# Expert products at one width: 64 slots as two times 32, and another order of the eight expert places

## The chip, the cores and the metric

The kernel runs on one core of a Trainium2 chip. The metric is device time in microseconds for one execution; the kernel before takes 1484.67 us as the median of three runs.

## The reference

A two-layer encoder trunk over 256 tokens of 1024 features, in f32, conditioned by one vector. Layer 0 has two kinds of attention side by side and a dense SwiGLU. Layer 1 has a dilated window attention and then eight routed experts, of which each token takes two. Only the experts matter here:

```python
logits = jnp.einsum('td,de->te', xt, router)
top_val, top_idx = lax.top_k(logits, 2)
gates = jax.nn.softmax(top_val, axis=-1)
...
xb = xt[tok]                                   # the tokens that chose expert e
yb = (jax.nn.silu(xb @ wg[e]) * (xb @ wu[e])) @ wd[e]     # 1024 -> 3584 -> 1024
...
y = jnp.zeros_like(xt).at[tok_pad].add(yb * g)
```

With 256 tokens and two choices each there are 512 token slots over eight experts, some 64 for each. The weights of one expert are 3 x 1024 x 3584 f32 values, 44 MB.

## The kernel before

The stages follow one another: modulation vectors, layer 0 attention, dense FFN, layer 1 projection (`project`, products 128 slots wide and 512 columns long that go to two PSUM banks in turn, three to each, through `mm3`, L331 to L333), dilated attention, routing, and from about 518 us the experts. The dense FFN of layer 0 uses `mm3` too, with 256 columns to a product.

The experts are worked off in eight **places**. Expert 7 (`FIRST`) is always in place 0. The other seven are ranked on the chip by how many tokens chose them, and `RANK` says which rank goes to which place. The three experts with the fewest tokens (ranks 0 to 2) have **small places**, with room for 64 slots (`TWO`); the other five have **large places**, with room for 96 (`ROOM`). Tokens beyond the room would go to `overflow`, behind a condition at the end (L1343 to L1356). The weights of a place are found with a register that holds the expert's number, so the program is the same for any routing.

Places are gathered in pairs (0,1), (2,3), (4,5), (6,7): `route` (L1234) builds one-hot matrices `oh`, multiplies the tokens `htok` by them (L1251) into `xg`, with the token slots of both places side by side, and makes the gates and row numbers for the way back (L1265 to L1268). The route of the next pair is written into the second place of a pair (`ahead`, in the code at the 18th of the down products).

Within a place the weights come as 42 slots of 1 MB, 28 for gate and up and 14 for down; each slot is two **granules** of 128 x 1024 values. SyncE issues the loads in the order of use. They go round a ring of 16 slots (`RING` 8, `RING2` 2, `RING4` 4, `RING3` 2); a load is issued when PE is done with the slot's granules before.

The token slots are PE's stationary operand and the weights the moving one. PE's array of 128 columns is split: a product of 64 token slots uses 64 of its columns, two such products (at `tile_position` 0 and 64) take two pieces of the granule; a product of 32 slots uses 32, and four of them (at 0, 32, 64, 96) take four pieces. `parts` (L1229) says that a small place is `(0, 64, 2)`, 64 slots in two pieces of 512 columns, and that a large place has `(64, 32, 4)` as well, the further 32 slots in four pieces of 256 columns. `products` (L1278) issues them granule by granule. The operands are f32; each product shows in the trace as two records, and each has its own weight load (PEld).

Gate and up have 7 groups of 8 granules (`for g`, `for k`). At the end of a group ScalarE (silu, L1310) and VectorE (product, L1311) make `hh`; `turn` (L1286) transposes it on PE (L1292, two transposes in a small place, three in a large one) and ScalarE and VectorE copy it to `ht` for the down products. In the code the turn of group g-1 stands after the fourth granule of group g. At the end of a place `scatter` (L1322) scales the result (L1327) and adds it to the output in DRAM by an indirect DMA from GpSimd (L1328): one for the first 64 slots, a second one for the further 32 of a large place. The two write the same output, so each waits for the one before.

The order on each engine isn't that of the code line by line: the framework that builds the program schedules ready instructions by priority, with its own assumptions on durations. The trace shows what came of it.

The modulation vectors come from `gemv_mm` (L311, products at L315): four products at a time, 32 columns of the array each, 512 columns of weights long.

Of the kernel before, what the change touches and what calls it, by code (L numbers as in the profile page):

```python
# [22 lines left out]
NE = 8  # L23
EPS = 1e-6
BIG = 4096.0
TWO = (1, 3, 5)
FIRST = NE - 1
RANK = (-1, 0, 3, 1, 4, 2, 5, 6)
ROOM = tuple(64 if j in TWO else 96 for j in range(NE))
RING = 8  # L30
NCONV = 3
# [148 lines left out]
def tile_trunk(ctx, tc, xT_d, fm_d, rw_d, ct_d, ada_et, ada_e, win_ab, win_c, uq_d, ukv_d, wout_e,  # L180
               ffn_gu, ffn_d, ada_ot, ada_o, qkv_d, wout_o, router_d, gu_d, wd_d, out, dbg=None):
    nc = tc.nc
    V, S, G, TE = nc.vector, nc.scalar, nc.gpsimd, nc.tensor
# [9 lines left out]
    def bank(tag):  # L193
        return psum.tile([P, 512], F32, tag=tag, name="ps" + tag, bufs={"A": 2, "D": 1, "B": 3, "C": 2}[tag])
# [40 lines left out]
    def F(n):  # L235
        return fm[:, FM[n][0]:FM[n][1]]
# [28 lines left out]
    for a in range(2):  # L265
        ps = bank("C")
        for b in range(4):
            k = 4 * a + b
# [490 lines left out]
    for a in range(3):  # L759
        g = F("qn")[:, a:a + 1] if a < 2 else F("kvn")  # L760
# [31 lines left out]
    for tt in range(2):  # L792
        for a in range(2):
            ps = bank("B")
# [6 lines left out]
    at = ExitStack()  # L801
# [88 lines left out]
    for f in range(22):  # L890
        ps = bank("A").rearrange("p (a b) -> p a b", a=2)
# [89 lines left out]
    at = ExitStack()  # L981
# [58 lines left out]
    def granules(j):  # L1040

        for make in [gu_load(j, g, kq) for g in range(7) for kq in range(4)] + [wd_load(j, pc) for pc in range(14)]:
            w = make()
            for lo in (0, 1024):
                yield w[:, lo:lo + 1024]
# [72 lines left out]
    rk8 = mb.tile([P, NE], F32, name="rk8")  # L1118
    for j, r in enumerate(RANK):
        G.memset(rt8[:, j:j + 1], float(r))  # L1120
# [3 lines left out]
    ps = bank("C")  # L1124
# [73 lines left out]
    def gates():  # L1198
# [14 lines left out]
        V.tensor_copy(eid, key)  # L1213
        V.tensor_scalar(cap, rk8, float(len(TWO)) - 0.5, -32.0, op0=ALU.is_lt, op1=ALU.mult)
        V.tensor_scalar(cap[:, :NR], cap[:, :NR], 96.0, None, op0=ALU.add)
# [13 lines left out]
    def parts(e):  # L1229


        return ((0, 64, 2),) if e in TWO else ((0, 64, 2), (64, 32, 4))

# [38 lines left out]
    def expert(e, xg, lo, mid, ahead):  # L1272


        wg = granules(e)
        hh, hts = {}, {}

        def products(outs, x, w, m, start, stop):  # L1278
            for ps, (at, n, q) in zip(outs, parts(e)):
                c = 1024 // m // q  # L1280
                wv = w.rearrange("p (m c) -> p m c", m=m)
                for j in range(q):
                    TE.matmul(ps[n * j:n * j + n, :m * c].rearrange("p (m c) -> p m c", m=m), x(at, n),  # L1283
                              wv[:, :, j * c:(j + 1) * c], start=start, stop=stop, tile_position=(0, n * j))

        def turn(g):  # L1286

            h = hh.pop(g)
            pt = bank("C")
            nb = 2 if e in TWO else 3  # L1290
            for b in range(nb):
                TE.transpose(pt[:, b * P:(b + 1) * P], h[:, b * P:(b + 1) * P], ident)  # L1292
            ht = mt.tile([P, 4, 96], F32, tag="ht%d" % g, name="ht")
            S.copy(ht[:, :, 0:64].rearrange("p (j b) t -> p b j t", b=2),  # L1294
                   pt[:, 0:256].rearrange("p (b j t) -> p b j t", b=2, j=2))
            if nb == 3:
                V.tensor_copy(ht[:, :, 64:96], pt[:, 256:384].rearrange("p (j t) -> p j t", j=4))  # L1297
            hts[g] = ht

        for g in range(7):  # L1300
            ps = [bank("A"), bank("B")][:len(parts(e))]
            for k in range(KD):
                products(ps, lambda at, n: xg[:, k, lo + at:lo + at + n], next(wg), 2, k == 0, k == KD - 1)
                if g and k == 3:
                    turn(g - 1)
                if g == 0 and k == 3 and mid:
                    mid()
            h = mt.tile([P, 384], F32, tag="hh", name="hh", bufs=2)
            for p, (at, w) in zip(ps, ((0, 256), (256, 128))):
                S.activation(h[:, at:at + w], p[:, 0:w], AF.Silu)  # L1310
                V.tensor_tensor(h[:, at:at + w], h[:, at:at + w], p[:, w:2 * w], op=ALU.mult)  # L1311
            hh[g] = h
        Y = [bank("D"), bank("B")][:len(parts(e))]
        for c in range(28):
            if c == 18 and ahead:
                ahead()
            products(Y, lambda at, n: hts[c // 4][:, c % 4, at:at + n], next(wg), 1, c == 0, c == 27)
            if c == 2:
                turn(6)
        return Y  # L1320
# [13 lines left out]
    for e in range(NE):  # L1334
        if e % 2 == 0:
            xg, at, back = nxt.pop()
        ahead = (lambda: nxt.append(route(e + 1))) if e % 2 and e + 1 < NE else None
        scatter(e, expert(e, xg, at[e % 2], None if e else g5_sum, ahead), back[e % 2])
# [104 lines left out]
```

## Time and profile before

| | |
|---|---|
| three runs | 1484.15, 1484.67, 1487.27 us; median 1484.67 |
| profiled execution | 1487.64 us; its span in the trace 1485.8 us |
| mean granted TensorE clock | 0.984 |
| PE products | 1418.4 us busy, 95% of the span, 9779 records |
| PE weight loads (PEld) | 647.5 us, 44%, 9779 records |
| VectorE, ScalarE, GpSimd | 433.6, 354.2, 51.1 us |
| read from HBM | 467.34 MB, mean 317 GB/s |

The profile shows one execution. Times of rows are microseconds from the start of the span; durations of single groups are in ns. PE is TensorE's products, PEld its weight loads, DVE VectorE, ACT ScalarE, POOL GpSimd, SP SyncE; a q behind it is the engine's sequencer. Products are pipelined, so a record is longer than the distance to the next one's start: the starts are what tells the pace. An x with a number is a count of records that a row merges.

### The profile page before, as it was taken

The page shows a single profiled execution, that of the slowest core. Times are in us where ns is not written, and L with a number is a line of the kernel's source. Part 1 is how long each engine was busy: PE and PEld are TensorE (multiplying, and loading weights), DVE is VectorE, ACT ScalarE, POOL GpSimd, SP SyncE. Part 2 cuts the span into 40 slices and gives each one's busy share as a digit, 9 for nine tenths or more (in the row PEclk, how much of TensorE's full clock was granted, in tenths as well). Part 3 has the DMA queues.
Part 4 walks back from the last instruction along what each step waited for, and adds up shares of the span by engine and source line. Part 5 has one row for each costly group of instructions (what it writes and reads, how often), then busy time and mean ns, then how long its engine had stood idle before and what let it go on. Part 6 is the DMA issues. An engine that isn't in the chain of part 4 may idle for free.

```text
span 1485.8 us, 23384 instructions
## 1 busy us (share of the span) xinstructions
PE 1418.4 (95%) x9779; PEld 647.5 (44%) x9779; DVE 433.6 (29%) x964; ACT 354.2 (24%) x750; POOL 51.1 (3%) x51
## 2 busy tenths in 40 slices
PE   6889999999989899999999998999998999999996
PEld 4646999998766722223322222322222322222221
DVE  5866787786886410000000000000000000000000
ACT  4557644445568310000100001100000100000000
POOL 0320000000020000000000000000000000000000
PEclk9989999999999899999999999999999999999998
DMA  9846678788432788999999999999999999999830
GB/s 393 341 155 251 212 285 299 284 306 308 161 114 91 295 336 321 320 331 415 421 418 420 378 331 419 421 417 421 351 333 410 421 414 421 367 326 335 317 140 11
DMA packets 67363, 472.11 MB, mean 318 GB/s; under 512 B 8145, under 2 KB 8593, under 8 KB 11185
## 3 DMA queue, kind: packets, MB, share of 16 engines
q1 hardware_dynamic: 64944, 467.34, 81.5%
q0 software_dynamic: 1872, 2.10, 0.9%
q8 instruction: 79, 1.29, 0.3%
q10 hardware_dynamic: 432, 1.08, 0.2%
q14 instruction: 36, 0.29, 0.1%
HBM read 467.34 MB, written 3.80 MB: 317 GB/s over the span
## 4 chain that ended last, share of the span: by engine, by line
issue 51%; PE 34%; DMA 7%; DVE 5%; ACT 2%; POOL 0%; POOLq 0%; SPq 0%; ACTq 0%; DVEq 0%
DMA out_dram<-acc,row 7%; PE psA L331 6%; PE psA L332 6%; PE psA L333 6%; PE psA L1283 4%; PE psB L1283 3%; PE psD L1283 2%; DVE wlo L355 1%; PE psD L610 1%; PE psB L315 1%; PE psC L596 1%; PE psB L562 1%; PE psA L562 1%; DMA w<-in_ada_ot_dram 1%; PE psC L1251 0%
## 5 line engine op out<-in xcount | busy, mean ns | idle before, releaser
L1283 PE MATMUL psA<-w,xg 128*64 128x512 f32 x1792 | 453.3, 612 | 0.0
L1283 PE MATMUL psD<-w,ht 128*64 128x512 f32 x896 | 229.3, 611 | 0.0
L1283 PEld LDWEIGHTS psA<-w,xg 128*64 128x64 f32 x1792 | 102.3, 136 | 196.9 <-issue 180.1
L1283 PE MATMUL psB<-w,xg 128*32 128x256 f32 x2240 | 180.8, 393 | 0.0
L1310 ACT ACTIVATE hh<-psA 128x256 f32<-128x256 f32 x56 | 21.5, 384 | 603.3 <-PE psA L1283 603.3
L355 DVE TENSOR_TENSOR wlo<-w,whi 128x1024 fp32r<-128x1024 f32 (+2 forms) x119 | 143.8, 1214 | 44.1 <-ACT whi L353 44.1
L1311 DVE TENSOR_TENSOR hh<-hh,psA 128x256 f32<-128x256 f32 x56 | 23.6, 421 | 452.2 <-ACT hh L1310 452.2
L1283 PEld LDWEIGHTS psB<-w,xg 128*32 128x32 f32 x2240 | 44.4, 108 | 227.7 <-issue 227.7
L353 ACT CAST whi<-w 128x1024 fp32r<-128x1024 f32 (+2 forms) x119 | 122.2, 1038 | 74.1 <-issue 30.0
L331 PE MATMUL psA<-h,whi 128*128 128x256 f32 x352 | 97.1, 277 | 0.2 <-ACT h L455 0.2
L332 PE MATMUL psA<-h,whi 128*128 128x256 f32 x352 | 97.1, 277 | 0.0
L333 PE MATMUL psA<-h,wlo 128*128 128x256 f32 x352 | 96.8, 276 | 0.0
L1283 PE MATMUL psB<-w,ht 128*32 128x256 f32 x1120 | 89.5, 391 | 0.0
L1283 PEld LDWEIGHTS psD<-w,ht 128*64 128x64 f32 x896 | 49.6, 135 | 90.2 <-issue 86.9
L1283 PEld LDWEIGHTS psB<-w,ht 128*32 128x32 f32 x1120 | 22.0, 108 | 113.6 <-issue 109.5
L1327 DVE SCALAR_TENSOR_TENSOR acc<-psD,gsl,g5a 128x512 f32<-128x512 f32 x8 | 6.0, 751 | 224.3 <-PE psD L1283 224.3
L331 PEld LDWEIGHTS psA<-h,whi 128*128 128x128 f32 x352 | 66.0, 188 | 0.6 <-ACT h L455 0.4
L332 PEld LDWEIGHTS psA<-h,whi 128*128 128x128 f32 x352 | 65.9, 188 | 0.3 <-DVE h L456 0.2
L333 PEld LDWEIGHTS psA<-h,wlo 128*128 128x128 f32 x352 | 65.9, 188 | 0.0
L1294 ACT COPY ht<-psC 128x256 f32<-128x256 f32 x56 | 20.9, 372 | 169.7 <-PE psC L1292 169.7
L1328 POOL DMA_INDIRECT out_dram<-acc,row x13 | 20.2, 1557 | 959.0 <-DVE acc L1327 923.4
L1297 DVE COPY ht<-psC 128x128 f32<-128x128 f32 x35 | 10.2, 292 | 141.6 <-ACT ht L1294 141.6
(335 smaller groups left out, 1583.5 us busy)
## 6 DMA issues: line engine op xcount, KB each, us to landing
w<-in_gu_dram SPq DMA_DIRECT2D x224, 1024.0 KB, 10.8
w<-in_wd_dram SPq DMA_DIRECT2D x112, 1024.0 KB, 11.1
w<-in_ada_e_dram SPq DMA_DIRECT2D x22, 1024.0 KB, 8.9
w<-in_ffn_gu_dram SPq DMA_DIRECT2D x22, 1024.0 KB, 5.1
w<-in_ada_ot_dram SPq DMA_DIRECT2D x16, 1024.0 KB, 4.9
w<-in_qkv_dram SPq DMA_DIRECT2D x12, 1024.0 KB, 6.6
w<-in_ffn_d_dram SPq DMA_DIRECT2D x11, 1024.0 KB, 6.6
w<-in_ada_o_dram SPq DMA_DIRECT2D x8, 1024.0 KB, 6.3
```

The costliest lines, as they stand in the source:

```text
L315: behind(TE.matmul(ps[32 * j:32 * j + 32], sc[:, 4 * i + j], w[:, j], start=i == 0, stop=i == 1, tile_position=(0, 32 * j)), after)
L331: TE.matmul(out_, a[0], b[0], start=start, stop=False)
L332: TE.matmul(out_, a[0], b[1], start=False, stop=False)
L333: TE.matmul(out_, a[1], b[0], start=False, stop=stop)
L353: behind(S.copy(hi[:, :n], w), self.after[0])
L355: self.last = V.tensor_tensor(lw, w, hi[:, :n].bitcast(F32), op=ALU.subtract)
L562: TE.matmul(bk[i][:, tt], q[:, tt * P:(tt + 1) * P], k, start=True, stop=True)
L1283: TE.matmul(ps[n * j:n * j + n, :m * c].rearrange("p (m c) -> p m c", m=m), x(at, n), wv[:, :, j * c:(j + 1) * c], start=start, stop=stop, ...
L1294: S.copy(ht[:, :, 0:64].rearrange("p (j b) t -> p b j t", b=2), pt[:, 0:256].rearrange("p (b j t) -> p b j t", b=2, j=2))
L1310: S.activation(h[:, at:at + w], p[:, 0:w], AF.Silu)
L1311: V.tensor_tensor(h[:, at:at + w], h[:, at:at + w], p[:, w:2 * w], op=ALU.mult)
L1328: G.indirect_dma_start(out=out.rearrange("t (j c) -> (t j) c", j=q), out_offset=bass.IndirectOffsetOnAxis(ap=row[:, 0:1], axis=0), in_=ys, ...
```

## The change

The small places move from 1, 3 and 5 to 1, 4 and 7. The ranks move with them, so that the three experts with the fewest tokens are still the ones in small places. In large places the first 64 slots are no longer multiplied as one product of 64 per piece, but as two products of 32 on the same piece of the weights, at neighbouring positions: four products of 512 columns at 0, 32, 64, 96, and then, as before, four of 256 columns. Small places keep their two products of 64. The turn of the group before stands one granule later in the code.

```diff
-TWO = (1, 3, 5)
+TWO = (1, 4, 7)
 FIRST = NE - 1
-RANK = (-1, 0, 3, 1, 4, 2, 5, 6)
+RANK = (-1, 0, 3, 4, 1, 5, 6, 2)
 ...
             for ps, (at, n, q) in zip(outs, parts(e)):
                 c = 1024 // m // q
                 wv = w.rearrange("p (m c) -> p m c", m=m)
+                b = n if e in TWO else 32
                 for j in range(q):
-                    TE.matmul(ps[n * j:n * j + n, :m * c].rearrange("p (m c) -> p m c", m=m), x(at, n),
-                              wv[:, :, j * c:(j + 1) * c], start=start, stop=stop, tile_position=(0, n * j))
+                    for i in range(0, n, b):
+                        o = n * j + i
+                        TE.matmul(ps[o:o + b, :m * c].rearrange("p (m c) -> p m c", m=m), x(at + i, b),
+                                  wv[:, :, j * c:(j + 1) * c], start=start, stop=stop, tile_position=(0, o))
 ...
-                if g and k == 3:
+                if g and k == 4:
                     turn(g - 1)
```

## Rows read from the trace of the kernel before

**Rows 1.** The page's list of engines: busy us, share of the span, records.
```profile
PE 1418.4 (95%) x9779; PEld 647.5 (44%) x9779; DVE 433.6 (29%) x964; ACT 354.2 (24%) x750; POOL 51.1 (3%) x51
```

**Rows 2.** Windows of places 0, 1, 2, 3, 7: length, busy, clock, DMA share, GB/s.
```profile
518.40:661.30 142.90, 142.90 (x1063) 33.99 (x1061) 10.04 (x31) 12.07 (x33) 0.00 (x0) 0.97 0.91 329
661.30:749.00 87.70, 83.32 (x420) 29.50 (x418) 4.66 (x16) 9.11 (x25) 3.27 (x2) 1.00 1.01 409
749.00:884.90 135.90, 135.90 (x1033) 31.96 (x1029) 8.23 (x23) 7.24 (x21) 1.54 (x1) 1.00 0.99 389
884.90:975.30 90.40, 83.19 (x418) 29.49 (x416) 4.70 (x16) 9.10 (x25) 3.09 (x2) 1.00 1.01 413
...
1337.60:1473.50 135.90, 135.90 (x1033) 31.97 (x1029) 8.10 (x24) 7.24 (x21) 3.09 (x2) 1.00 0.61 215
```

**Rows 3.** Waits of PE and PEld, 661 to 1474 us: total us, times, longest.
```profile
PE psC L1292 <- DVE hh L1311: 15.1, 16, 0.9
...
PEld psA L1283 <- DMA w<-in_gu_dram: 3.8, 12, 0.4
```

**Rows 4.** Timeline of PE in place 2: start, length, instruction, records merged.
```profile
761.56 1.08 PE L1283 MATMUL psA<-w,xg 128*64 128x512 f32 x4
...
762.04 0.60 PE L1283 MATMUL psA<-w,xg 128*64 128x512 f32 x2
...
762.57 0.64 PE L1283 MATMUL psB<-w,xg 128*32 128x256 f32 x8
...
762.80 0.40 PE L1283 MATMUL psB<-w,xg 128*32 128x256 f32 x4
763.13 1.08 PE L1283 MATMUL psA<-w,xg 128*64 128x512 f32 x4
764.14 0.64 PE L1283 MATMUL psB<-w,xg 128*32 128x256 f32 x8
764.71 0.55 PE L1292 MATMUL psC<-fm,hh 128*128 128x128 f32 x3
765.19 1.08 PE L1283 MATMUL psA<-w,xg 128*64 128x512 f32 x4
```

**Rows 5.** Timeline of PE in place 3, the first group and its transposes.
```profile
884.87 7.09 PE L1283 MATMUL psA<-w,xg 128*64 128x512 f32 x32
892.90 0.44 PE L1292 MATMUL psC<-fm,hh 128*128 128x128 f32 x2 [0.94 <-DVE hh L1311]
```

**Rows 6.** Timeline of PE in the layer-1 projection, across a change of bank.
```profile
360.16 0.39 PE L333 MATMUL psA<-whi,h 128*128 128x512 f32 x1
360.38 0.39 PE L331 MATMUL psA<-whi,h 128*128 128x512 f32 x1
```

**Rows 7.** Timeline of PE in the modulation products ahead of the experts.
```profile
501.93 2.78 PE L315 MATMUL psA<-w,sc 128*32 128x512 f32 x24
```

**Rows 8.** Timeline of PE, the gathering among the down products of place 3.
```profile
948.17 0.79 PE L1251 MATMUL psC<-oh,htok 128*128 128x160 f32 x5
...
950.76 0.79 PE L1251 MATMUL psC<-oh,htok 128*128 128x160 f32 x5
```

**Rows 9.** Windows within place 1: with scatters under way, and after them.
```profile
661.30:673.00 11.70, 11.70 (x59) 3.87 (x57) 1.08 (x3) 0.76 (x2) 1.73 (x1) 1.00 0.96 333
...
700.00:749.00 49.00, 46.35 (x248) 17.70 (x250) 2.00 (x10) 5.69 (x16) 0.00 (x0) 1.00 1.01 421
```

**Rows 10.** The chain that ended last, and the timeline of POOL, at the end.
```profile
1474.09 5.85 DMA out_dram<-acc,row
...
1480.69 1.54 POOL L1328 DMA_INDIRECT out_dram<-acc,row  x1 [5.06 <-DMA out_dram<-acc,row]
```

**Rows 11.** Windows in the dense FFN and late in place 5: records of PE, PEld.
```profile
211.00:225.00 14.00, 14.00 (x126) 14.00 (x126) 11.06 (x18) 6.80 (x11) 0.00 (x0) 1.00 0.80 285
...
1188.90:1193.10 4.20, 4.03 (x64) 1.89 (x60) 0.47 (x3) 1.28 (x5) 0.00 (x0) 1.00 1.02 423
```

## The prediction

> **What bounds the kernel now.** I read the busy times first: PE works 95% of the span, no other engine a third of it [rows 1]. Then the expert stage by windows, one window for each of the eight places. The places follow one another without gaps from 518.4 to 1473.5 us, 955 of the 1485.8 us, and they come in two kinds. A large place (0, 2, 7, and 4 and 6 like them) takes 135.9 us, place 0 with its start 142.9; a small one (1, 3, and 5 like it) takes 87.7 or 90.4 [rows 2]. In large places PE is busy from end to end and the weights arrive at 389 GB/s or less, in place 7 at 215, because nothing is left to load; in small places they arrive at 409 to 413. So I looked at who waits: in the whole stage PE waits for weights a few times for 0.4 us, and in small places some 16 times 0.9 us for the activations in front of a transpose [rows 3]. The bound is PE, and in a large place it is PE's own stream.
>
> Next that stream. A granule is one half of a loaded slot (128 rows by 1024 columns, 0.524 MB). A large place passes it as two products 64 slots wide and 512 columns long, then four products 32 wide and 256 long; each product shows as two records. The first records start at 761.56, the second pair at 762.04, the 32-wide ones at 762.57, their second four at 762.80, the next granule at 763.13 [rows 4]. PE's granted clock is 1.00 in all places but the first (0.97) [rows 2]. So products at different column positions run together ("a round"), and the four rounds of a granule last 0.48, 0.53, 0.23 and 0.33 us: 1.57 us.
>
> Now the same 64-wide products in a small place, where nothing else is between them: 32 records, 16 rounds, take 7.09 us; less the 0.6 us of the last record that is 0.43 us for a round [rows 5]. So a round of 512 columns that costs 0.43 in an even stream costs 0.48 and 0.53 in a large place. The loss stands where the width changes. What else changes there is the PSUM bank. But in the layer-1 projection the bank changes after every third product, at equal width (128), and the next one starts the usual 0.22 us later, between a third product (L333) and the next first (L331) [rows 6]. Hence the width.
>
> **The change: the stream of the five large places.** After it, all products of a large place are 32 wide: per granule two rounds of four with 512 columns and two rounds of four with 256. Is a round of four as quick as a round of two? The modulation products (L315) are just that, 32 wide, 512 long, four positions: 24 records, six rounds, take 2.78 us [rows 7]; less 0.6 for the last record that is 0.43 a round. So 2 x 0.43. A 256-column round in an even stream isn't in the trace. Lower bound: half of 0.43, 0.215; upper bound: 0.24, rounded up from the 0.23 of the first round of a pair, which holds a restart [rows 4]. I take 0.215, because rounds scale with columns (512 columns cost 0.43 both at two and at four positions). Granule: 0.86 + 0.43 = 1.29 us, with the upper bound 1.34.
>
> The transposes (turn) still change the width, once into them and once out. In a large place they stand after the second granule of the next group, not after the fourth where the code has them: 764.71 to 765.19, 0.48 us, after 0.57 for a pair of 256 rounds that started at 764.14 [rows 4]; 0.57 less 0.24 and 0.215 leaves 0.1 for the change of width. Today one of the two changes happens anyway; afterwards neither does, so a turn costs 0.48 + 0.1 + 0.03 for the restart (0.24 - 0.215), say 0.62, instead of 0.49 (764.14 to 765.19 is 1.05, an ordinary pair to the next granule 0.56). A large place today: (135.9 - 7 x 0.49)/84 = 1.577 us per granule. Afterwards: 84 x 1.29 + 7 x 0.62 = 112.7 us. That saves 23.2 us in each of five, 116 us. The start of place 0 stays: 142.9 - 23.2 = 119.7.
>
> **turn at k == 4 instead of 3.** It can only matter where the order on the engine follows the code. In large places it doesn't, as seen, and in small places the transposes stand right behind the eighth granule and wait 0.94 us for hh [rows 5]. I cost it at nothing; hidden by one more granule of products. If that order moves so that large places also wait, it is 0.94 x 7 x 4 = 26 us.
>
> **The order of the places.** PE's sum is unchanged by it: three small, five large. The gathering for the next pair (route, five products of 128 columns per two granules, 948.17 to 950.76 = 2.59 us against 1.72 for two granules bare, eight times) [rows 8] stays in places 1, 3 and 5, of which 3 and 5 become large. So a large place with it takes 112.7 + 7 = 119.7, a small one without it 90.4 - 7 = 83.4. The exchange is nil.
>
> What the order does is to spread the weight traffic. The ring holds 16 slots of 1.05 MB. With the queue never refused the weights come at 421 GB/s, with the output's scatters between them at 333 for 12 us [rows 9], and 409 to 413 as the mean of a small place [rows 2]; I take 410. A place eats 84 x 0.524 = 44.0 MB. Full ring less what is in flight, about 14.7 MB, at the end of place 0 (638.1 us). Then: place 1 (small, 87.7 us) 36.0 in: 6.7 left. Place 2 (112.7) 46.2 in: 8.9. Place 3 (119.7) 49.1: 14.0. Place 4 (small, 83.4) 34.2: 4.2. Place 5 (119.7): 9.3. Place 6 (112.7): 11.5. Place 7 (small) 34.2: 1.7 MB. It never reaches zero, but it ends near it. The other way round: 7 x 44.0 - 14.7 = 293.6 MB at 410 GB/s is 716 us, last landing near 1354, and PE's sum ends at 1473.5 - 116 = 1357.5. The two lines run within 4 us of each other, so from here PE and weights bound the kernel together; for their meeting I add 2 us: 1359.5. With the old order the ring would drop 8 MB in each of places 1, 3 and 5 and win back 2 between, and run dry in place 5.
>
> **The tail.** Place 7 today ends with two scatters, one behind the other: the first is issued at 1474.09 and under way for 5.85 us, the second not before 1480.69, the span ends at 1485.8 [rows 10]. A small place last has only the first part. From PE's end to the first scatter it is then some 1.2 us instead of 0.6 (no 32-wide products run behind the last 512 columns), 5.9 for the scatter, and for what follows the last landing I take 1.7, a third of the 5.1 from the second issue to the end: 8.8 us instead of 12.3.
>
> **Sum.** 1359.5 + 8.8 = 1368.3 of span. The profiled run was 1487.64 beside a span of 1485.8: 1370.1. It lay 3.0 above the median of the three runs, so against the median: 1367 us, 7.9% faster.
>
> **The rivals.**
> *Instructions (slower).* PE gets its instructions too slowly for the finer split. A granule becomes 32 records of PE (16 loads, 16 products) instead of 24, in 1.29 us: one every 40 ns. The densest long stretch of the trace is 126 + 126 in 14 us, 56 ns each [rows 11]. If that were the pace at which PE gets its instructions, a granule would take 1.78 us, 0.20 more than today over 420 granules: 85 us slower, with the shorter tail 1566. It decides from 49 ns on (1.577/32). Against it: 64 + 60 records in 4.2 us near the end of place 5, 34 ns each [rows 11], and that long stretch has a load and a product of 256 columns every 111 ns, while 512 columns take 0.22 us [rows 6], so columns set its pace. Chance 0.06.
> The Trainium skill (TensorE: Matmul & The Clock Gate, section "Wait — 56ns, not 53.3ns?") has about 62 ns for a matmul where the sequencer decodes it in software; by that, four products of a 256 round would take 0.25 us and a granule 1.36, some 28 us more in all. The trace speaks against it: the four records of a second round take 0.40 us together [rows 4], so they start nearly at once. I give it 0.01, and 1395 lies within the range.
> *Four at 512 columns don't run together while weights stream* (only two read at a time). The round then doubles to 0.86, a granule takes 2.15 us, 240 us slower. In the modulation products four run together [rows 7]; 0.01, counted with the slower side.
> *The weights become the bound alone.* If four streams of PE push the queue to 390 GB/s, the 293.6 MB take 753 us: last landing 1391, time 1401. For it: the ring's ledger ends at 1.7 MB; against it: 421 GB/s beside PE's densest small place. Chance 0.07.
> *The order on the engine moves* and the transposes of large places wait as in the small ones, or 256 rounds stay at 0.24: 21 to 26 us more, 1388 to 1393. Chance 0.11.
> *No gain, the pauses belong to something else than width.* Then only the tail stays: 1481. The even step over a bank change speaks against it [rows 6]: 0.02.
>
> **How the numbers follow.** The forecast holds 0.72, the others 0.28, its own range 1358 to 1380 (down: DMA at 421 where no scatter stands and rounds at 0.427; up: a few us of empty ring in each small place). The range goes from 1355 to 1398: it takes in the moved order and most of the weight bound, and leaves out about 0.12. A measurement of this kernel tells some 0.2% from nothing. Slower than that only by the first two rivals, 0.07; within it 0.01; faster 0.92.
>
> **What would show it.** Right: in large places records of 32 columns alone, rounds 0.43 and 0.22 us apart, granules 1.29 us, the place 113 us; GB/s above 400 from place 1 to the end; PE's first real waits for weights, if any, late in places 4 and 7; one scatter at the end. Wrong: granules over 1.4 us with weights landed (instructions or reading); waits for w in many places (the queue); transposes with idle time before them in large places (the order).

## The result and the profile after

The changed kernel takes 1366.36 us, the median of four runs (1362.31 to 1370.07), beside 1485.93 for the kernel before (four runs, 1484.15 to 1487.27): a ratio of 0.9195, 95% interval 0.9161 to 0.9230. The forecast was 1367 us. The profiled run of after took 1363.57 us with a span of 1361.7, so it lies 2.8 under its median, while that of before lay 3.0 over its own.

The page's list of engines, of after (before: [rows 1]):
```profile
PE 1301.8 (96%) x11459; PEld 718.2 (53%) x11459; DVE 430.8 (32%) x964; ACT 354.4 (26%) x750; POOL 51.1 (4%) x51
```
The 1680 records that PE has more are the added products (420 granules of large places, two products more each, two records to a product), and still PE is busy 117 us less. VectorE, ScalarE and GpSimd have not moved by 3 us.

The eight places of after by windows, in the columns of [rows 2]: length, busy time and records of PE, PEld, DVE, ACT, POOL, then granted clock, share of the DMA engines, GB/s.
```profile
516.40:635.20 118.80, 118.80 (x1395) 46.92 (x1393) 9.22 (x31) 11.95 (x33) 0.00 (x0) 0.98 0.99 388
635.20:721.80 86.60, 83.62 (x438) 29.31 (x435) 5.17 (x17) 9.46 (x26) 3.27 (x2) 1.00 1.01 417
721.80:834.50 112.70, 112.70 (x1371) 45.15 (x1373) 7.32 (x23) 7.23 (x21) 1.54 (x1) 1.00 1.01 419
834.50:955.30 120.80, 120.74 (x1434) 53.62 (x1426) 8.80 (x31) 11.03 (x32) 3.09 (x2) 1.00 1.01 412
955.30:1037.25 81.95, 76.31 (x353) 24.83 (x351) 3.77 (x9) 5.29 (x14) 3.09 (x2) 1.00 1.01 416
1037.25:1157.60 120.35, 120.29 (x1426) 50.12 (x1428) 7.59 (x25) 11.03 (x32) 1.54 (x1) 1.00 1.01 419
1157.60:1270.80 113.20, 113.20 (x1375) 46.45 (x1367) 7.79 (x24) 7.23 (x21) 3.09 (x2) 1.00 1.02 417
1270.80:1353.80 83.00, 76.41 (x354) 24.82 (x350) 3.81 (x9) 5.29 (x14) 3.09 (x2) 1.00 0.93 383
```
Three things are to be seen. A large place without gathering (2, 6) now takes 112.7 to 113.2 us where [rows 2] show 135.9. The weights arrive at 412 to 419 GB/s from place 1 to place 6, where large places had 389 and less before. And the places still add up without a gap, from 516.4 to 1353.8, 2 us earlier at the start than in the profiled run of before.

Inside a large place, the timeline of PE in place 2 of after (start, length, instruction, records merged):
```profile
775.87 1.04 PE L1286 MATMUL psA<-w,xg 128*32 128x512 f32 x8
776.72 0.61 PE L1286 MATMUL psB<-w,xg 128*32 128x256 f32 x8
777.16 1.04 PE L1286 MATMUL psA<-w,xg 128*32 128x512 f32 x8
...
778.01 0.61 PE L1286 MATMUL psB<-w,xg 128*32 128x256 f32 x8
778.56 0.55 PE L1295 MATMUL psC<-fm,hh 128*128 128x128 f32 x3
779.04 1.07 PE L1286 MATMUL psA<-w,xg 128*32 128x512 f32 x8
779.92 0.61 PE L1286 MATMUL psB<-w,xg 128*32 128x256 f32 x8
```
Read by starts: two rounds of 512 columns in 0.85 us (775.87 to 776.72), two of 256 in 0.44, a granule in 1.29 (775.87 to 777.16). Where the transposes stand, the pair of 256 rounds before them is 0.55 long instead of 0.44, they themselves 0.48, and the pair of 512 rounds behind them 0.88 instead of 0.85: a turn costs 0.62 us, the value in the forecast.

The waits of PE and PEld from 516 to 1354 us, of after (total us, times, longest), which answer to [rows 3]:
```profile
PE psC L1295 <- DVE hh L1314: 14.1, 15, 0.9
...
PEld psA L1286 <- DMA w<-in_gu_dram: 4.6, 16, 0.3
```
The waits before transposes are still the only ones of any size: some 15 of 0.9 us, as before.

How near the weights are can be worked out from the windows: length times GB/s is what came in, and a place uses 42 x 1.0486 = 44.04 MB. From place 1 on 36.1, 47.2, 49.8, 34.1, 50.4, 47.2 and 31.8 MB came, 296.6 in all (the small change of other transfers included), against 308.3 used. So 11.7 MB were in the ring when place 1 began, and at the ends of the places it held 3.7, 6.9, 12.7, 2.7, 9.1, 12.3 and 0 MB. The forecast's ledger was 6.7, 8.9, 14.0, 4.2, 9.3, 11.5, 1.7. PE's end and the queue's meet in place 7. (The zero there is the assumption that nothing is loaded beyond need; the other levels follow from it. By windows the queue still moves 198 GB/s from 1345 to 1350 us and 18 from there to 1354, so the last weights land some 4 us before PE is done with them.)

The tail, from the timelines of VectorE and GpSimd of after (in square brackets: idle time before, and what ended it), against [rows 10]:
```profile
1353.89 0.75 DVE L1330 SCALAR_TENSOR_TENSOR acc<-psD,gsl,g5a 128x512 f32<-128x512 f32 x1 [24.73 <-PE psD L1286]
...
1354.91 1.54 POOL L1331 DMA_INDIRECT out_dram<-acc,row  x1 [71.93 <-DVE acc L1330]
```
One scatter, issued 1.1 us after PE's end; the span ends at 1361.7.

### The profile page after: what moved, and what is told of

Same layout as the page of the kernel before. It is cut to its first block, busy times and chain, and to the rows that moved or that the text cites. A ratio compares the mean times of both kernels' runs of the same rounds, so it can differ in the third digit from the quotient of the medians.

```text
span 1361.7 us, 26744 instructions
## 1 busy us (share of the span) xinstructions
PE 1301.8 (96%) x11459; PEld 718.2 (53%) x11459; DVE 430.8 (32%) x964; ACT 354.4 (26%) x750; POOL 51.1 (4%) x51
## 4 chain that ended last, share of the span: by engine, by line
PE 86%; DVE 6%; issue 3%; ACT 3%; DMA 1%; POOL 0%; POOLq 0%; SPq 0%; ACTq 0%; DVEq 0%
PE psA L1286 28%; PE psD L1286 15%; PE psB L1286 13%; PE psA L331 7%; PE psA L332 6%; PE psA L333 6%; PE psC L1295 2%; PE psC L1251 2%; DVE wlo L355 1%; PE psD L610 1%; PE psB L315 1%; DMA w<-in_wd_dram 1%; PE psC L596 1%; PE psB L562 1%; PE psA L562 1%
## 5 line engine op out<-in xcount | busy, mean ns | idle before, releaser
L1286 PE MATMUL psA<-w,xg 128*32 128x512 f32 (+1 forms) x2912 | 448.8, 596 | 0.0
L1286 PE MATMUL psD<-w,ht 128*32 128x512 f32 (+1 forms) x1456 | 227.9, 594 | 0.0
L1286 PEld LDWEIGHTS psA<-w,xg 128*32 128x32 f32 (+1 forms) x2912 | 119.3, 116 | 139.9 <-issue 90.6
L1286 PEld LDWEIGHTS psB<-w,xg 128*32 128x32 f32 x2240 | 74.6, 110 | 164.1 <-issue 162.3
L355 DVE TENSOR_TENSOR wlo<-w,whi 128x1024 fp32r<-128x1024 f32 (+2 forms) x119 | 143.9, 1215 | 47.2 <-ACT whi L353 47.2
L1286 PEld LDWEIGHTS psD<-w,ht 128*32 128x32 f32 (+1 forms) x1456 | 62.9, 116 | 64.6 <-issue 41.7
L1286 PE MATMUL psB<-w,ht 128*32 128x256 f32 x1120 | 95.1, 379 | 0.0
L1286 PEld LDWEIGHTS psB<-w,ht 128*32 128x32 f32 x1120 | 40.1, 110 | 77.6 <-issue 75.1
```

The source lines that it names most:

```text
L355: self.last = V.tensor_tensor(lw, w, hi[:, :n].bitcast(F32), op=ALU.subtract)
L1286: TE.matmul(ps[o:o + b, :m * c].rearrange("p (m c) -> p m c", m=m), x(at + i, b), wv[:, :, j * c:(j + 1) * c], start=start, stop=stop, til ...
```

## Experiments

**The parts alone.** The first four ran on one chip, with the kernel before beside them at 1487.19 us.

E1, the 32-wide products without the new order of places:
```diff
-TWO = (1, 4, 7)
+TWO = (1, 3, 5)
-RANK = (-1, 0, 3, 4, 1, 5, 6, 2)
+RANK = (-1, 0, 3, 1, 4, 2, 5, 6)
...
-                if g and k == 4:
+                if g and k == 3:
```


> The 32-wide products alone; places and turn as in the kernel before. Width theory: large places still 113 us, so PE's own work is that of the changed kernel; but the small places at 1, 3 and 5 empty the ring (some 6 slots lost in each, 1 to 2 won back in a large one), PE waits for weights some 10 us in places 3 to 6, and the second scatter is back (3.5): 1376 to 1386 us. Rival, the order of the places is worth only the scatter: 1369 to 1371. Rival, the order and not the width made the gain: 1470 to 1486.

Measured: 1379.19 us (1377.31 to 1381.06), ratio 0.9272 (0.9249 to 0.9294). The width alone brings 108 of the 120 us. Place 5 of E1, the third small one, by windows, and the waits for weights in it:
```profile
1037.00:1137.80 100.80, 87.99 (x438) 28.69 (x437) 5.01 (x14) 9.48 (x26) 3.09 (x2) 0.98 1.02 419
```
```profile
PEld psA L1286 <- DMA w<-in_gu_dram: 16.1, 15, 1.4
...
PE psA L1286 <- DMA w<-in_gu_dram: 5.0, 9, 0.8
```
With gathering a small place took 90.4 us before [rows 2]; this one takes 100.8, with the queue at its full 419 GB/s and PE and its weight loads waiting for weights up to 1.4 us at a time. (Its granted clock is 0.98 and not 1.00; by that figure I estimate that up to 2 of the 10.4 us are the clock's.) In the old order the ring does run dry in place 5, as the ledger said. And two scatters stand at E1's end again: its last 256-column products start at 1363.50 and are over by 1364.1, and the span ends at 1377.0, a tail of 13 us.

E2, the order alone (64-wide products kept):
```diff
-TWO = (1, 3, 5)
+TWO = (1, 4, 7)
-RANK = (-1, 0, 3, 1, 4, 2, 5, 6)
+RANK = (-1, 0, 3, 4, 1, 5, 6, 2)
```


> The new order of places alone, first 64 slots one product of 64 again, turn at 3. Width theory: only the second scatter at the end goes, 3 to 4 us: 1481 to 1483, ratio 0.9975. Rival, the order carries part of the gain by itself: under 1475.

Measured: 1480.69 us (1477.79 to 1485.02, ten runs), ratio 0.9959 (0.9942 to 0.9975): about 6 us, not 3.5. Two of its places by windows (3, large with gathering; 4, small without), and its last instruction on GpSimd:
```profile
884.60:1026.70 142.10, 142.04 (x1097) 37.35 (x1093) 9.34 (x31) 11.05 (x32) 3.09 (x2) 1.00 0.90 313
1026.70:1109.60 82.90, 76.32 (x356) 24.98 (x354) 3.67 (x9) 5.30 (x14) 3.09 (x2) 1.00 1.01 410
```
```profile
1471.85 1.54 POOL L1328 DMA_INDIRECT out_dram<-acc,row  x1 [72.28 <-DVE acc L1327]
```
PE ends at 1470.8 and the span at 1478.5, so the tail is 7.7 us, not the 8.8 that I had put together. And the gathering costs a large place 142.1 - 135.9 = 6.2 us, while a small place without it is 90.4 - 82.9 = 7.5 us shorter: the exchange, which I had called nil, gains 1.3 us for each of the two. The tail's 4.6 (12.3 before) and these 2.6 make 7 us, within the interval of the ratio, which is 3.7 to 8.6 us.

E3, the change with the turn at its old place:
```diff
-                if g and k == 4:
+                if g and k == 3:
```


> The changed kernel with the turn back behind the fourth granule. Theory: nothing within 3 us of the changed kernel (1363 to 1370), because in most places the transposes don't stand where the code has them. Rival, the later turn saves waits for hh: 5 to 26 us slower.

Measured: 1365.80 us (1363.89 to 1367.08), ratio 0.9181 (0.9159 to 0.9203). The later turn does nothing that can be told. By the order of the records it moves only 13 of the 56 turns, by one granule each: six in place 0, three in place 1, four in place 6.

Since E1 and E3 differ in the order of places alone and ran side by side, the order is worth 13.4 us beside the new width, and only 6 beside the old one: besides a tail that is 5 us shorter it takes away the dry ring, which the old width never had.

**Is it the width?** E4, also on that chip, gives small places four 32-wide products as well, so that all eight places have one width:
```diff
-                b = n if e in TWO else 32
+                b = 32
```


> Small places too take their 64 slots as two times 32. Theory: four 512-long products at a time cost what two cost, a round stays 0.43 us, a granule 0.86 us in small places; 1362 to 1372. Rival, four at a time read or issue more slowly and the large places hide it behind something else: a granule of a small place over 0.95 us, 1385 and more.

Measured: 1367.39 us (1363.32 to 1370.87), ratio 0.9190 (0.9164 to 0.9216). The same six granules in place 4, first of E4, then of after (timeline of PE):
```profile
966.66 5.36 PE L1286 MATMUL psA<-w,xg 128*32 128x512 f32 x48
```
```profile
964.40 5.37 PE L1286 MATMUL psA<-w,xg 128*64 128x512 f32 x24
```
48 records of four products at a time take what 24 records of two do. Neither the narrower product nor the number of instructions has a price here; for the same slots, four at a time are no faster than two either. So what the change won in large places isn't won by "four at once".

E5 takes the kernel before, 64-wide products and all, and only puts the two granules of a slot together: first the 64-wide products of both, then the 32-wide ones of both (gate and up; the down products likewise). That halves the changes of width and keeps every instruction.
```diff
-        def products(outs, x, w, m, start, stop):
-            for ps, (at, n, q) in zip(outs, parts(e)):
+        def products(outs, x, w, m, start, stop, only):
+            for ps, (at, n, q) in list(zip(outs, parts(e)))[only:only + 1]:
...
-            for k in range(KD):
-                products(ps, lambda at, n: xg[:, k, lo + at:lo + at + n], next(wg), 2, k == 0, k == KD - 1)
+            for k2 in range(0, KD, 2):
+                ws = [next(wg), next(wg)]
+                for p in range(len(ps)):
+                    for k, w in zip((k2, k2 + 1), ws):
+                        products(ps, lambda at, n: xg[:, k, lo + at:lo + at + n], w, 2, k == 0, k == KD - 1, p)
```


> The kernel before, but its large places pass the 64-wide products of both granules of a slot and then the 32-wide ones of both, so that the width (and the bank) changes half as often. Width theory: 0.29 us less for every second granule, a slot 2.87 instead of 3.15 us, 420/2 x 0.29 = 61 us: 1421 to 1428. Rival, the pauses come with each load of a 64-wide product after another bank's rounds only at the start of a slot or with the weights' semaphore: no change, 1484 to 1488.

Measured (the kernel before at 1487.21 beside it): 1430.81 us (1425.08 to 1432.46), ratio 0.9613 (0.9588 to 0.9638). Place 2 of E5 by windows, and one slot of it in the timeline of PE:
```profile
737.60:862.50 124.90, 124.90 (x1032) 40.24 (x1028) 8.51 (x23) 7.22 (x21) 1.54 (x1) 1.00 1.01 418
```
```profile
800.99 1.94 PE L1283 MATMUL psA<-w,xg 128*64 128x512 f32 x8
802.86 1.07 PE L1283 MATMUL psB<-w,xg 128*32 128x256 f32 x16
```
The slot takes 1.87 + 1.00 = 2.87 us (its next product starts at 803.86), where two granules took 3.15 and now take 2.58. One pair of changes instead of two: 0.28 less; none: 0.57 less. The loss goes with the number of changes, about 0.29 us for a change and the change back. The large place comes to 124.9 us, between 135.9 and 112.7; the midpoint would be 124.3. Five times 11.0 us are 55 and not the 61 of the expectation, and the time lies 3 us above the 1421 to 1428 expected.

Together with the width, E5 halves the changes of PSUM bank and of column count. The changed kernel still has both in every granule (psA with 512 columns, psB with 256), and there they cost nothing: 0.85 and 0.44 us, as shown above. That leaves the width. The weight loads show what is different at a change of width (timeline of PEld, first two lines of before, then two of after):
```profile
761.55 0.20 PEld L1283 LDWEIGHTS psA<-w,xg 128*64 128x64 f32 x4 [0.41 <-issue]
...
762.56 0.16 PEld L1283 LDWEIGHTS psB<-w,xg 128*32 128x32 f32 x8 [0.81 <-issue]
```
```profile
775.65 0.35 PEld L1286 LDWEIGHTS psA<-w,xg 128*32 128x32 f32 x8
776.30 0.13 PEld L1286 LDWEIGHTS psB<-w,xg 128*32 128x32 f32 x4 [0.30 <-issue]
```
In before the loads behind a change begin with the products themselves: 761.55 and 762.56, beside products that start at 761.56 and 762.57 [rows 4]. In after, across the same change of bank, they begin a round ahead: 775.65 for products at 775.87, 776.30 for products at 776.72. It is so at every step between psA or psD and psB in place 2, by the starts of the records: at most 0.003 us ahead in before, 0.21 or 0.43 us in after. So no load runs ahead across a change of width; that this alone makes up the 0.28 us isn't shown.

**What binds now.** E6 leaves out the slots from 64 on in all large places (their products, transposes and scatters), to see how early the weights alone let the kernel end:
```diff
-        return ((0, 64, 2),) if e in TWO else ((0, 64, 2), (64, 32, 4))
+        return ((0, 64, 2),)
```
(with all places at 64-wide products and two transposes to a turn.)

> The changed kernel without the work on slots 64 to 95 of large places (their products, transposes and scatters are left out); all places as small ones, 64 wide, the ring and all loads as they are. PE has some 180 us less to do. Theory, weights bound right behind PE: 336 slots at 2.5 us less what the ring holds at the start end near 1335, 1340 to 1352 us. Rival, PE alone was the bound: 1190 to 1220.

Measured: 1347.73 us (1346.88 to 1352.62), ratio 0.9072 (0.9049 to 0.9094). Its expert stage by windows, first the stretch that is place 0 in the changed kernel and then the rest, and the waits of PE in it:
```profile
516.00:635.00 119.00, 110.76 (x501) 35.80 (x500) 7.38 (x19) 12.65 (x32) 1.72 (x1) 0.98 1.01 420
635.00:1338.00 703.00, 561.34 (x2464) 161.04 (x2466) 26.24 (x66) 45.88 (x122) 9.25 (x6) 1.00 1.01 416
```
```profile
PE psA L1286 <- DMA w<-in_gu_dram: 67.2, 111, 1.4
...
PE psD L1286 <- DMA w<-in_wd_dram: 30.3, 53, 1.4
```
PE is idle for 150 of 822 us, the queue works at 416 to 420 GB/s throughout, and only 18.6 us are gone. About half of them come from place 0, where the changed kernel's queue ran at 388 GB/s: 118.8 x (420 - 388)/417 = 9.1 us. So behind place 0 the changed kernel stands within some 10 us of what the weights allow.

E7 takes the other bound away. Half of each slot is loaded; PE multiplies by that half twice, and the other half of the weights is left out.
```diff
-            return lambda: load(gu_d[FIRST, g, kq].rearrange("p a b c -> p (a b c)"), (2048,))
+            return lambda: load(gu_d[FIRST, g, kq][:, 0:1].rearrange("p a b c -> p (a b c)"), (1024,))
...
-            for lo in (0, 1024):
+            for lo in (0, 0):
```


> The changed kernel with half of every expert slot loaded (1024 of 2048 values; PE multiplies the first granule twice, so the second granule's weights are left out). PE does what it did, the queue half. Theory, PE and weights bind nearly together: PE's own sum remains, 1354 to 1366 us. Rival, weights alone were the bound: under 1330.

Measured: 1342.29 us (1339.99 to 1345.27), ratio 0.9028 (0.9008 to 0.9048). That is below the 1354 to 1366 of the theory and above the 1330 of its rival: both missed. Its places 4 and 7 by windows and, from place 4, the timeline of PE; then the same stretch of after:
```profile
950.00:1025.90 75.90, 75.90 (x352) 24.82 (x350) 3.79 (x9) 5.30 (x14) 3.09 (x2) 1.00 0.86 288
1257.50:1333.40 75.90, 75.90 (x354) 24.82 (x350) 3.83 (x9) 5.29 (x14) 3.09 (x2) 1.00 0.58 194
```
```profile
961.70 7.09 PE L1286 MATMUL psA<-w,xg 128*64 128x512 f32 x32
968.71 0.44 PE L1295 MATMUL psC<-fm,hh 128*128 128x128 f32 x2
```
```profile
970.71 0.44 PE L1295 MATMUL psC<-fm,hh 128*128 128x128 f32 x2 [0.94 <-DVE hh L1314]
971.08 7.09 PE L1286 MATMUL psA<-w,xg 128*64 128x512 f32 x32
```
Place 4 takes 75.9 us instead of 82.0: with other load sizes the framework has put the transposes elsewhere, behind the fifth granule of the next group, and they find `hh` ready. So this run changed two things at once, the loads and the order on PE; E9 tells them apart. What it does tell by itself: with neither waits nor weights in its way, PE ends the kernel near 1342, and the waits before transposes are a real part of PE's chain there.

E9 asks for those waits alone. It is the changed kernel with an order-only dependency that holds the transposes of a turn behind the last product of the granule after which the code has them:
```diff
-                TE.transpose(pt[:, b * P:(b + 1) * P], h[:, b * P:(b + 1) * P], ident)
+                behind(TE.transpose(pt[:, b * P:(b + 1) * P], h[:, b * P:(b + 1) * P], ident), after)
...
-                products(ps, lambda at, n: xg[:, k, lo + at:lo + at + n], next(wg), 2, k == 0, k == KD - 1)
+                mm = products(ps, lambda at, n: xg[:, k, lo + at:lo + at + n], next(wg), 2, k == 0, k == KD - 1)
...
-                    turn(g - 1)
+                    turn(g - 1, mm)
```


> The changed kernel with the transposes held behind the fifth granule, where the code has them, in every place (for the last group behind the third down granule), so that PE no longer waits 0.94 us for hh in small places. Theory, the weights end only 2 us before PE, so what PE wins it then waits for weights: 1361 to 1366, at most 3 us of the 17 that go. Rival, PE's waits in small places count in full: 1347 to 1352.

Measured (the kernel before at 1485.75 beside it): 1365.26 us (1362.57 to 1369.51), ratio 0.9197 (0.9176 to 0.9217). Places 4 and 7 of E9 by windows, and the waits of PE for weights from 516 to 1354 us:
```profile
951.90:1031.20 79.30, 76.87 (x352) 24.68 (x351) 4.38 (x10) 5.30 (x14) 3.09 (x2) 1.00 1.02 416
...
1265.60:1352.40 86.80, 79.41 (x354) 23.56 (x350) 3.81 (x9) 5.30 (x14) 3.09 (x2) 1.00 0.93 380
```
```profile
PE psD L1286 <- DMA w<-in_wd_dram: 5.7, 11, 0.7
...
PE psA L1286 <- DMA w<-in_gu_dram: 1.2, 3, 0.6
```
The waits for `hh` are gone, place 4 is 2.7 us shorter, and place 7 is 3.8 us longer, with PE now waiting for weights. The time is that of the changed kernel, which the same chip ran again as E11. Late in place 7 the timeline of PE shows the pace:
```profile
1330.75 1.94 PE L1286 MATMUL psD<-w,ht 128*64 128x512 f32 x8 [0.55 <-DMA w<-in_wd_dram]
1333.24 1.94 PE L1286 MATMUL psD<-w,ht 128*64 128x512 f32 x8 [0.55 <-DMA w<-in_wd_dram]
```
A slot is used up every 2.49 us, and 1.0486 MB in 2.49 us are 421 GB/s: the weights set the pace. E7 has the same order on PE: by the records all 56 turns of the two runs stand at the same granule, and only the gathering among the down products of places 1, 3 and 5 stands otherwise. So the 23 us between 1342.29 and 1365.26 are in the main those of the loads: place 7 takes 75.9 us with half of them and 86.8 with all. A wait of PE costs nothing here while the ring is about to run dry anyway.

**A larger ring.** E8 gives the changed kernel a 17th slot (and one less of the small `gsl` and `row` buffers); E10 is E9 with the same; E11 is the changed kernel once more, without an edit.
```diff
-RING3 = 2
+RING3 = 3
...
-                gsl = mt.tile([P, 1], F32, tag="gsl", name="gsl", bufs=8)
+                gsl = mt.tile([P, 1], F32, tag="gsl", name="gsl", bufs=7)
```


> The changed kernel with 17 slots in the ring instead of 16 (room made by one buffer less of two tiny tiles). If the weights bind from place 1 on, one slot more that is loaded ahead is one slot's time, 2.5 us: 1361 to 1366, at the edge of what can be told. If PE binds: no change.

> The same with 17 slots in the ring. Theory, the weights bind: 2.5 us more than with 16: 1358 to 1364. Rival, PE binds: as e9.

> The changed kernel again, beside the two on the same chip: 1363 to 1369.

Measured: E8 1365.03 us (1364.35 to 1366.88), ratio 0.9183 (0.9169 to 0.9196), beside E5 to E7; E10 1363.42 (1360.30 to 1365.09), ratio 0.9166 (0.9148 to 0.9185); E11 1365.45 (1363.08 to 1369.49), ratio 0.9193 (0.9172 to 0.9214). One slot is worth 2.5 us of loading, and a difference of that size can't be told apart here: E8 is inconclusive, and E10, the lowest of the changed kernel's relatives that compute everything, overlaps with E11. Whether forced transposes and a larger ring together gain 2 us stays open.

## Why the prediction was right, point by point

*The width.* The loss between 64-wide and 32-wide products is the change of width. E5 halves the changes and gains half; the changed kernel keeps the changes of bank and of column count and loses nothing by them; E4 shows that narrowness by itself does nothing. The two rounds of 512 columns take 0.85 us (taken: 0.86), the two of 256 take 0.44 (taken: 0.43, the lower of its two bounds), the granule 1.29, the turn 0.62, the place 112.7: these terms are as forecast. Place 0 has 118.8 (119.7), places 3 and 5 have 120.8 and 120.4 (119.7), 4 and 7 have 82.0 and 83.0 (83.4), place 1 has 86.6 (87.7).

*The turn at k == 4.* Nothing, as costed (E3).

*The order of the places.* The ledger held: 3 MB less in the ring at the start than put down, but the same course, to zero in place 7; and the old order runs dry in place 5 (E1). The exchange of gathering between large and small places came out nil in the changed kernel (places 3 and 5 are 1.1 and 0.7 above their term, 4 and 7 are 1.4 and 0.4 below), though beside the old width it gained 2.6 us (E2). What was off is the 2 us for the meeting of PE and weights, which were not needed. PE ends at 1353.8 instead of 1359.5: 2.0 of that is the earlier start of the stage, 2 the meeting, 1.7 the sum of the places.

*The tail* was put at 8.8 us and is 7.9 (E2 has 7.7).

*The sum* for the profiled run was 1370.1, and it took 1363.57, 6.5 less: 5.7 by PE's end and 0.9 by the tail. That the median comes within 1 us of 1367 is in part luck: the correction of 3.0 from profiled run to median went the other way in after, whose profiled run was quicker than its median.

*The rivals.* The pace of instructions is refuted. A stretch of place 2 of after, by windows:
```profile
800.00:814.00 14.00, 14.00 (x179) 5.69 (x175) 0.29 (x1) 0.37 (x1) 0.00 (x0) 1.00 1.01 420
```
It has 354 records of PE and PEld in 14 us, one every 39.5 ns, where the rival needed 49 or more. By the prediction's estimate the rule of the Trainium skill (TensorE: Matmul & The Clock Gate, section "Wait — 56ns, not 53.3ns?"), about 62 ns for a matmul decoded in software, would have made the granule 1.36 us. It is 1.29, so the rounds do not show that rule. On the mean the products of this stretch start 78 ns apart (14 us by 179), so no run here tells whether 62 ns would bind as a mean. Four products of 512 columns run together while the weights stream at 420 GB/s. The weights did not fall to 390 GB/s beside four streams of PE. The transposes of large places did not begin to wait: in place 2 PE is busy for all of its 112.70 us. (The 26 us for that rival count four large places; with all five they would have been 33.) And that the pauses belong to something else than the width is excluded by E5 together with the changed kernel's own stream.

What I had not foreseen is how the two bounds share the end. I treated PE's waits of 0.94 us in small places as part of PE's sum, and they are; but E9 shows that taking them away only moves the wait to the weights. From here less work for PE alone brings at most the 18.6 us of E6, half of them in place 0; taking PE's waits away alone brings nothing that can be told (E9); half the loads, with those waits gone too, brought 24 us (E7). For the order that the framework chose when the loads changed (E7) I have no cause, only the trace.

## What to carry to other kernels

On TensorE, keep the products of one stream at one width of column tile: here each change between 64 and 32 columns and back cost some 0.29 us, 0.57 of the 3.15 us of a slot, though PE looked busy throughout. Read a pipelined engine by the distance between starts, and compare the same instruction in an even and in a mixed stream before believing a busy share of 95%. When the main engine becomes 8% faster, write the ledger of the next bound (what comes in and what is used, place by place): it said here that the work which lets the ring fill must be spread out, and it says now that a wait of PE is free where the ring is nearly empty.

## What the runs showed of the hardware beyond that

The four column positions need not keep step. In place 3 of after, behind the gathering, the rounds no longer stand in line (timeline of PE):
```profile
944.77 1.02 PE L1286 MATMUL psD<-w,ht 128*32 128x512 f32 x5
945.27 0.38 PE L1286 MATMUL psB<-w,ht 128*32 128x256 f32 x1
945.28 0.62 PE L1286 MATMUL psD<-w,ht 128*32 128x512 f32 x2
...
946.06 1.02 PE L1286 MATMUL psD<-w,ht 128*32 128x512 f32 x5
```
A record doesn't name its position, but the single starts fall into four chains, each with steps of 0.43 and 0.43 us from its two 512-column records and 0.22 and 0.22 from its two 256-column ones, and I read the chains as the positions. Some are already at their 256-column products (945.27) while others still start 512-column ones (945.28), and the granule is 1.29 us all the same (944.77 to 946.06). So, read this way, at equal width a position need not wait for the others, while at a change of width, by the starts in [rows 4] and by E5, time is lost.
